# The order of the last query/key chunk and the third quarter's units in local attention

## The chip, the cores and the metric

The kernel runs on one core of a Trainium2 chip. The metric is the device time of one execution in microseconds, taken as the median over several runs. A core has TensorE (matrix products and transposes into PSUM), VectorE (DVE), ScalarE (ACT), GpSimd (POOL) and SyncE (SP). Each engine works through its own instruction list in order, and waits on semaphores for the others. Loads and stores are issued from SP's or GpSimd's queue and run on 16 shared DMA engines.

## The reference, cut to what matters

The program is a two-layer encoder trunk on 512 tokens of width 1024: a dilated sliding-window attention layer, a gated MLP, a gated linear attention layer, another MLP. The change touches the attention layer alone. It has three groups of 16 heads of width 64, with window and dilation (128, 1), (512, 4), (2048, 16):

```python
qkv = (h @ w_in).reshape(bsz, seq, A_N_GROUPS, 3, A_HEADS, A_HEAD_DIM)
for g, (window, dilation) in enumerate(A_GROUPS):
    q = rope(rms_norm(qkv[:, :, g, 0], q_gain[g]), positions)
    k = rope(rms_norm(qkv[:, :, g, 1], k_gain[g]), positions)
    o, lse = dilated_window_attention(q, k, qkv[:, :, g, 2], window, dilation)
    ...
alpha = jax.nn.softmax(jnp.stack(lses, axis=0), axis=0)
out = jnp.sum(alpha[..., None] * jnp.stack(outs, axis=0), axis=0)
return out.reshape(bsz, seq, A_WIDTH) @ w_out
```

So for each head the three groups' results are weighted by their softmax denominators, summed, and projected by `w_out`.

## The kernel before

**Quarters.** The heads are taken in four quarters of four heads. First the two dilated groups are computed for all four quarters (`attend_dilated`); their results go to DRAM. Then the local group (window 128, dilation 1) is computed for quarters 0 to 3, combined with the dilated results, and projected. The change is in this second part, in `attention` (L834 to L860).

**A query/key chunk, QK0 to QK3** (`qk_chunk`, L558). Each computes query and key of one quarter for all 512 tokens. `chunk_of` (L533) loads four weight tiles of 512 KB on SP's queue (L103), splits each in two parts on ScalarE and VectorE (L96, L97), and multiplies: 8 steps of the width, 4 token tiles, 3 products each (L547 to L549), so 96 matmuls of 512 columns into four PSUM accumulators (tag "pp", four in all). Then, token tile by token tile, ScalarE copies the accumulator to a "zs" buffer (L569) and squares it (L571), VectorE sums (L572), scales and rotates it (L585 to L590) and transposes 32x32 blocks into another "zs" buffer (L591). Sixteen transfers on SP's queue (L595) put the blocks in place in a third "zs" tile, and four ScalarE copies (L604) make the operands. There are only two "zs" buffers:

```python
"zq": 3, "qk": 8, "v": 8, "zs": 2,
```

so a tile takes its place when the tile before in that buffer has been read for the last time. QK0 to QK2 end in "zq" buffers, QK3 in four "qk" ones.

**A value chunk** (`v_chunk`, L608). For quarters 0 and 1 there is one chunk of 512 columns, and for quarters 2 and 3 a half chunk each: V2 and V3, two weight loads and 96 matmuls of 256 columns, into the same four "pp" accumulators; ScalarE copies them out (L616).

**The units, U0 to U3** (`attend_local`, L748). A quarter has four units (two pairs of heads, two pairs of token tiles). A unit is: 8 score matmuls (L767); on VectorE masking and minimum (L625); on ScalarE the exponentials (L626); 8 transposes on TensorE (L638); copies out (L656); and 16 matmuls with the values (L678). The last of these are given out one unit later (`weigh_pending`, L681). The pair's result is copied, turned back (L696), combined with the dilated one on VectorE (`combine`, L778) and turned once more (L696) to be an input of the projection, again some units later. GpSimd loads the dilated results (L751, L754) and clears borders (L628, L630).

**The output projection** (`out_attention`, L869). Its first half needs the outputs of quarters 0 and 1 (8 output tiles of 4 steps, 96 matmuls of 512 columns, L108 to L110, weights `a_w_out`), its second half also those of quarters 2 and 3. The outputs of quarters 0 and 1 are split into "xs" buffers (L852), which are those of the layer's normalized input; so the splits wait until V3, the last reader of that input, has passed.

**What sets the order.** The program is written as one sequence. A planner in the language lays it out as one list per engine before anything runs: place in the written sequence is priority, an instruction whose inputs the planner expects later is passed by later ones that it holds ready, and weight loads with their splits are given a place some hundred instructions ahead (`high_priority(offset=AHEAD)`, L103 to L105). On the chip the lists are fixed. So work that is written behind a quarter's units fills TensorE between them.

Of the kernel before, what the change touches and what calls it, by code (L numbers as in the profile page):

```python
# [39 lines left out]
class Trunk:  # L40
# [793 lines left out]
    def attention(self):  # L834
        self.masks = None
        self.pending = None
        self.later = []
        with self.phase("attn", self.ATTN):
            self.ready = self.first_tiles()
            far = [self.attend_dilated(u) for u in range(4)]  # L840
            self.load_x("xT", 64)
            qk = [self.qk_chunk("qk", 0)]
            v = [self.v_chunk(self.ins["a_w_v0"], 8)] * 2
            self.o = []
            self.inputs_read = False
            for u in range(2):
                qk.append(self.qk_chunk("qk", u + 1))
                self.attend_local(u, *qk[u], v[u], *far[u])
            for u in (2, 3):
                v.append(self.v_chunk(self.ins["a_w_v0b"][u - 2], 8, 256))  # L850
                if u == 3:
                    self.o = [self.split(e, (P, S), "xs", "xs") for e in self.o]  # L852
                    self.inputs_read = True
                self.attend_local(u, *qk[u], v[u], *far[u])
                if u == 2:
                    qk.append(self.qk_chunk("qk", 3))
            while self.pending or self.later:
                self.run_later()
                self.weigh_pending()
            self.load_h(self.ins["xT"], None)  # L860
# [363 lines left out]
```

## Time and profile before

| what | before |
|---|---|
| median of three runs | 1502.98 us (1502.92 to 1504.03) |
| the profiled execution | 1505.45 us |
| its span, first to last instruction | 1503.7 us |
| granted TensorE clock over the span | 0.994 |
| TensorE busy | 1473.7 us |
| VectorE / ScalarE / GpSimd busy | 964.3 / 785.5 / 110.2 us |

The span is the time between the first and the last instruction of the profiled execution; some 2 us lie around it. Times in rows of the profile are counted from the span's start. In rows of engines, the first number is the start, the second the length, "L" the line of the kernel, then what is written and read, shapes, and the number of instructions put together; in brackets stands how long the engine had stood idle, and what released it. "PE" is TensorE. In groups, behind the bar, stand the total busy time in us and the mean in ns, then the idle time before.

### The profile page before, as it was taken

How to read it: one execution, taken by the hardware profiler on the slowest of the kernel's cores; microseconds unless marked ns; L12 is line 12 of the kernel's file. 1: busy time of each engine (PE TensorE's matmuls, PEld its weight loads, DVE VectorE, ACT ScalarE, POOL GpSimd, SP SyncE). 2: the span in 40 equal slices, each digit the busy share in tenths (PEclk: the TensorE clock that was granted, in tenths of full speed). 3: DMA queues.
4: the chain of work that ended last, by engine and by line, in shares of the span. 5: the costliest groups of instructions: out<-in, count | busy, mean ns of one | idle time of the engine just before them, and what ended most of it. 6: DMA issues, size and time to landing. Idle time of an engine off the chain costs nothing.

```text
span 1503.7 us, 21140 instructions
## 1 busy us (share of the span) xinstructions
PE 1473.7 (98%) x7950; PEld 1209.9 (80%) x7950; DVE 964.3 (64%) x1756; ACT 785.5 (52%) x1352; POOL 110.2 (7%) x192
## 2 busy tenths in 40 slices
PE   8999999999999979999999999999999999999998
PEld 6877878777787857788888887888888888889887
DVE  6585858687775847866667334947576866668222
ACT  6334454555566355765567223556644855568121
POOL 0001010101001001111110000000010211110000
PEclk9999999999999989999999999999999999999999
DMA  8644443444333327777674333212155776675331
GB/s 275 180 126 109 123 115 95 137 145 102 110 95 106 76 68 207 224 167 154 147 157 131 99 97 99 87 56 85 50 159 184 198 168 153 156 152 148 121 107 60
DMA packets 87477, 196.53 MB, mean 131 GB/s; under 512 B 13104, under 2 KB 38256, under 8 KB 87376
## 3 DMA queue, kind: packets, MB, share of 16 engines
q1 hardware_dynamic: 72560, 145.77, 31.7%
q0 software_dynamic: 14816, 49.42, 16.2%
q8 instruction: 62, 1.02, 0.3%
q14 instruction: 39, 0.32, 0.1%
HBM read 174.11 MB, written 8.46 MB: 121 GB/s over the span
## 4 chain that ended last, share of the span: by engine, by line
PE 73%; DVE 12%; ACT 4%; DMA 4%; issue 4%; SPq 2%; POOL 0%; DVEq 0%; ACTq 0%; POOLq 0%
PE ppp L109 8%; PE ppp L108 8%; PE ppp L110 8%; PE ppp L328 6%; PE ppp L330 6%; PE ppp L329 6%; PE ppp L547 5%; PE ppp L548 5%; PE ppp L549 5%; DVE wl L97 3%; PE ps L329 2%; PE ps L330 2%; PE ps L328 2%; SPq L595 2%; PE po L678 2%
## 5 line engine op out<-in xcount | busy, mean ns | idle before, releaser
L96 ACT ACTIVATE wh<-wf 128x1024 fp32r<-128x1024 f32 (+1 forms) x184 | 191.3, 1041 | 340.8 <-PE ppp L109 187.0
L97 DVE TENSOR_TENSOR wl<-wf,wh 128x1024 fp32r<-128x1024 f32 (+1 forms) x184 | 220.4, 1199 | 206.7 <-ACT wh L96 206.1
L547 PE MATMUL ppp<-wh,xs 128*128 128x512 f32 (+1 forms) x672 | 259.1, 386 | 7.5 <-ACT wh L96 5.4
L548 PE MATMUL ppp<-wl,xs 128*128 128x512 f32 (+1 forms) x672 | 257.7, 384 | 0.1
L549 PE MATMUL ppp<-wh,xs 128*128 128x512 f32 (+1 forms) x672 | 256.3, 382 | 0.0
L547 PEld LDWEIGHTS ppp<-wh,xs 128*128 128x128 f32 x672 | 126.8, 189 | 36.4 <-ACT zs L569 5.7
L548 PEld LDWEIGHTS ppp<-wl,xs 128*128 128x128 f32 x672 | 126.9, 189 | 25.6 <-issue 2.0
L549 PEld LDWEIGHTS ppp<-wh,xs 128*128 128x128 f32 x672 | 127.0, 189 | 24.5 <-issue 0.8
L97 DVE TENSOR_TENSOR wl<-wA,wh 128x1024 fp32r<-128x1024 f32 x88 | 107.4, 1222 | 33.8 <-ACT wh L96 33.6
L96 ACT ACTIVATE wh<-wA 128x1024 fp32r<-128x1024 f32 x88 | 93.1, 1059 | 58.1 <-PE ppp L330 37.9
L328 PE MATMUL ppp<-wh,a 128*128 128x512 f32 (+1 forms) x288 | 109.1, 384 | 1.9 <-DVE h L867 1.9
L329 PE MATMUL ppp<-wl,a 128*128 128x512 f32 (+1 forms) x288 | 108.0, 375 | 0.0
L330 PE MATMUL ppp<-wh,a 128*128 128x512 f32 (+1 forms) x288 | 108.0, 376 | 0.0
L109 PE MATMUL ppp<-xs,wh 128*128 128x512 f32 x272 | 106.5, 393 | 0.0
L110 PE MATMUL ppp<-xs,wl 128*128 128x512 f32 x272 | 105.4, 390 | 1.1 <-DVE wl L97 1.1
L108 PE MATMUL ppp<-xs,wh 128*128 128x512 f32 x272 | 105.5, 392 | 0.5 <-ACT xs L96 0.5
L97 DVE TENSOR_TENSOR wl<-wB,wh 128x1024 fp32r<-128x1024 f32 x38 | 46.6, 1225 | 76.0 <-ACT wh L96 76.0
L626 ACT ACTIVATE sm<-sm,st 128x160 f32<-128x160 f32 (+2 forms) x128 | 56.9, 446 | 38.0 <-DVE st L625 37.9
L328 PE MATMUL ps<-wh,sh 128*128 128x512 f32 (+1 forms) x192 | 72.9, 381 | 0.0
L328 PE MATMUL ppp<-wh,sh 128*128 128x512 f32 (+1 forms) x192 | 72.2, 376 | 0.0
L329 PE MATMUL ps<-wl,sh 128*128 128x512 f32 (+1 forms) x192 | 71.7, 373 | 0.0
L329 PE MATMUL ppp<-wl,sh 128*128 128x512 f32 (+1 forms) x192 | 71.5, 372 | 0.1
(325 smaller groups left out, 2928.3 us busy)
## 6 DMA issues: line engine op xcount, KB each, us to landing
wA<-in_gate_up_dram POOLq DMA_DIRECT2D x52, 512.0 KB, 6.1
wf<-in_down_dram SPq DMA_DIRECT2D x32, 512.0 KB, 3.5
wf<-in_gate_up_dram SPq DMA_DIRECT2D x24, 512.0 KB, 5.2
wf<-in_a_w_v_dram SPq DMA_DIRECT2D x20, 512.0 KB, 3.9
wB<-in_gate_up_dram POOLq DMA_DIRECT2D x20, 512.0 KB, 5.6
wf<-in_a_w_q_dram SPq DMA_DIRECT2D x16, 512.0 KB, 4.0
zq<-zs SPq DMA_DIRECT2D x128, 64.0 KB, 2.1
wf<-in_a_w_qk_dram SPq DMA_DIRECT2D x16, 512.0 KB, 4.3
```

Of the source, the lines that this page charges most:

```text
L96: nc.scalar.activation(hi, src, AF.Copy)
L97: self.low = nc.vector.tensor_sub(lo, src, hi.bitcast(F32))
L108: mm(out, lhsT=wh, rhs=xh, start=start, stop=False)
L109: mm(out, lhsT=wh, rhs=xl, start=False, stop=False)
L110: self.multiplied = mm(out, lhsT=wl, rhs=xh, start=False, stop=stop)
L328: mm(a, lhsT=xh[:, tok], rhs=wh[:, f], start=start and k == 0, stop=False, skip_group_check=True)
L329: mm(a, lhsT=xh[:, tok], rhs=wl[:, f], start=False, stop=False, skip_group_check=True)
L330: self.multiplied = mm(a, lhsT=xl[:, tok], rhs=wh[:, f], start=False, stop=k == last, skip_group_check=True)
L547: mm(a, lhsT=xh, rhs=wh[:, f], start=k == 0, stop=False)
L548: mm(a, lhsT=xh, rhs=wl[:, f], start=False, stop=False)
L549: self.multiplied = mm(a, lhsT=xl, rhs=wh[:, f], start=False, stop=k == KT - 1)
L626: nc.scalar.activation(sm[:, w], sm[:, w], AF.Exp, bias=n, scale=-1.0, accum_out=l)
```

## The change

In the local part the written order of chunks and units is another. Before: QK0, V0/V1, then QK1, U0, QK2, U1, then V2, U2, QK3, V3, U3. After: QK0, V0/V1, then QK1, U0, QK2, U1, QK3, V2, U2, V3, U3. The four loop passes have one form: next query/key chunk, the half value chunk for quarters 2 and 3, the units. No instruction is added or removed.

```diff
             v = [self.v_chunk(self.ins["a_w_v0"], 8)] * 2
             self.o = []
             self.inputs_read = False
-            for u in range(2):
-                qk.append(self.qk_chunk("qk", u + 1))
-                self.attend_local(u, *qk[u], v[u], *far[u])
-            for u in (2, 3):
-                v.append(self.v_chunk(self.ins["a_w_v0b"][u - 2], 8, 256))
+            for u in range(4):
+                if u < 3:
+                    qk.append(self.qk_chunk("qk", u + 1))
+                if u > 1:
+                    v.append(self.v_chunk(self.ins["a_w_v0b"][u - 2], 8, 256))
                 if u == 3:
                     self.o = [self.split(e, (P, S), "xs", "xs") for e in self.o]
                     self.inputs_read = True
                 self.attend_local(u, *qk[u], v[u], *far[u])
-                if u == 2:
-                    qk.append(self.qk_chunk("qk", 3))
```

## The prediction

> **What bounds the kernel now.** I read the top of the profile's page first, then the waits of TensorE over the whole span.
>
> ```profile
> span 1503.7 us, 21140 instructions
> PE 1473.7 (98%) x7950; PEld 1209.9 (80%) x7950; DVE 964.3 (64%) x1756; ACT 785.5 (52%) x1352; POOL 110.2 (7%) x192
> ```
>
> ```profile
> PE ps L638 <- ACT sm L626: 7.1, 5, 4.7
> ...
> PE ps L767 <- ACT qk L604: 2.0, 1, 2.0
> ...
> PE ppp L110 <- DVE wl L97: 1.1, 1, 1.1
> ```
>
> TensorE is the bound: 1473.7 of 1503.7 us. An edit that only changes the order can win no more than its idle time and what it loses to a lowered clock. The columns of the waits are total us, times, longest. The longest single line of that list, 7.1 us, is a transpose of attention probabilities (L638) that waits for its exponentials (L626); next to it stand the first local scores (L767) that wait for a copied query and key (L604). Both lie in the part of the kernel that the change reorders. Here is that part by stretches: length, then busy us of TensorE, its weight loads, VectorE, ScalarE, GpSimd, then the granted TensorE clock.
>
> ```profile
> core 0: us, PE busy (x) PEld busy (x) DVE busy (x) ACT busy (x) POOL busy (x), PEclk, DMA share, GB/s
> 427.70:463.30 35.60, 35.13 (x279) 29.59 (x277) 30.87 (x96) 25.37 (x67) 2.34 (x8) 1.00 0.31 74
> 463.30:491.50 28.20, 27.84 (x203) 21.34 (x201) 13.24 (x53) 19.92 (x55) 2.65 (x10) 1.00 0.27 92
> 491.50:503.80 12.30, 12.30 (x101) 12.15 (x100) 12.10 (x32) 7.89 (x17) 0.99 (x3) 1.00 0.09 23
> 503.80:527.20 23.40, 22.27 (x98) 17.77 (x96) 17.23 (x29) 3.88 (x5) 0.00 (x0) 1.00 0.47 114
> 527.20:561.60 34.40, 25.80 (x187) 20.22 (x187) 16.19 (x61) 19.99 (x53) 1.44 (x6) 0.80 0.21 68
> ...
> 582.00:600.00 18.00, 17.66 (x68) 13.83 (x69) 15.46 (x25) 11.86 (x19) 1.05 (x2) 0.91 0.57 143
> 600.00:640.00 40.00, 38.48 (x173) 30.34 (x173) 35.38 (x53) 28.95 (x43) 7.82 (x12) 1.00 0.72 210
> ```
>
> With the names of the text above (QK = query/key chunk, V = value chunk, U = the four local units of a quarter): the first stretch is U1 with V2 and the start of QK3 between its units; the second is U2 with the rest of QK3; the third is V3 alone; the fourth is the first half of the output projection, all 96 of its matmuls; the fifth is U3. U1 and U2 keep TensorE at 99%, because other matmuls run while a unit's softmax is on VectorE and ScalarE. U3 does not: it loses 34.40 - 25.80 = 8.60 us, and its clock is 0.80.
>
> Why U3 has nothing to run beside it is in the time at which QK3 becomes usable. Four rows of TensorE, two of ScalarE (start, length, line), and the transfer issues of SP:
>
> ```profile
> 427.60 0.39 PE L549 MATMUL ppp<-wh,xs 128*128 128x512 f32 x1
> ...
> 492.07 0.40 PE L549 MATMUL ppp<-wh,xs 128*128 128x512 f32 x1
> ...
> 529.15 1.65 PE L767 MATMUL ps<-qk,qk 64*128 64x192 f32 x8 [1.99 <-ACT qk L604]
> 535.46 1.97 PE L638 MATMUL ps<-ident,sm 128*128 128x128 f32 x8 [4.66 <-ACT sm L626]
> ```
>
> ```profile
> 462.98 2.19 ACT L604 ACTIVATE zq<-zs 128x512 f32<-128x512 f32 x4 [0.38 <-DMA zs<-zs]
> ...
> 527.43 2.19 ACT L604 ACTIVATE qk<-zs 128x512 f32<-128x512 f32 x4 [8.21 <-DMA zs<-zs]
> ```
>
> ```profile
> 438.54 2.02 SPq L103 DMA_DIRECT2D wf<-in_a_w_qk_dram  x2
> 450.64 10.77 SPq L595 DMA_DIRECT2D zs<-zs  x16
> 461.52 1.01 SPq L103 DMA_DIRECT2D wf<-in_a_w_v0b_dram  x2
> 470.49 42.86 SPq L103 DMA_DIRECT2D wf<-in_a_w_out_dram  x5
> 514.84 10.94 SPq L595 DMA_DIRECT2D zs<-zs  x16
> ```
>
> From a chunk's last matmul to its last copy is one long chain: norm, rotation, sixteen SP transfers, four copies. For QK2 it runs from 427.99 to 465.17 (37.2 us), for QK3 from 492.47 to 529.62 (37.2 us again). Behind QK3's last matmul stand only V3 and the projection's first half, 12.3 + 23.4 = 35.7 us. They are spent as cover for the chain, and are missing when U3 comes.
>
> **The change part by part.** It removes and adds no instruction. It moves QK3 (4 weight loads, 96 matmuls, its ScalarE and VectorE chain, 16 transfers, 4 copies) from behind U2 to ahead of V2 and U2; V2 moves behind QK3, and V3 stays ahead of U3. I take its effect in the order of time.
>
> *U1.* Its filler was V2 and a part of QK3; now it is QK3.
>
> ```profile
> L547 PE MATMUL ppp<-wh,xs 128*128 128x256 f32 x32 | 9.2, 292 | 0.1
> ...
> L547 PE MATMUL ppp<-wh,xs 128*128 128x512 f32 x13 | 5.2, 399 | 0.0
> ```
>
> These are the first of three equal lines (L547, L548, L549) in 427.7 to 463.3: V2's 96 matmuls and 39 of QK3's. V3's like 96 fill the third stretch with four others, so a half value chunk is about 11.5 us. The projection's 96 of 512 columns, with two others, are the 22.27 us busy of the fourth stretch, so QK3 is about 22 us, and its 39 are 9 us. U1 took 11.5 + 9 = 20.5 us of filler; QK3 has 22. So U1 runs as before, and QK3 ends some 1.5 us behind U1, at about 464.8. Cost: nothing, with QK3 as the work that hides it; if that cover were gone, U1 would look like U3.
>
> *The hand-over from QK3 to V2.* All four accumulators of QK3 must be copied out (L569) into a "zs" buffer before V2 can start. There are two such buffers; the one QK3 needs is held until QK2's sixteen transfers have landed, at about 462.6 by the row that ends at 461.41 and the copies that start at 462.98. QK3 ends at 464.8, 2 us later. The same hand-over from QK2 to V2 before cost well under 0.5 us (the first stretch idles 0.47 us in all). I put 0.5 us on it, between 0 and 2.2 (one set of four copies, as in L604's row).
>
> *U2.* QK3's chain is now beside U2, as QK2's was beside U1: VectorE was busy 30.87 of 35.60 us there, and 13.24 of 28.20 in U2. So U2 gets U1's pace, 35.6 us in place of 28.2, and takes U1's 20.5 us of filler. There are V2 and V3, 23 us. U2 ends near 500.4; V3's last 2.5 us bring TensorE to about 503, and QK3's copies end at 464.8 + 37.2 = 502.0. The work of TensorE from 427.7 to 503.8 is the same set of instructions as before, and it stood still for only 0.83 us in it, so this point comes at 503.8 again, give or take 0.5.
>
> *U3.* Its scores are now ready when V3 ends, and the projection's first half (22 us) and 24 matmuls of its second (5 to 6 us) can go between its units and behind the last. U2 took 59 matmuls, 13.5 us, at the pace of a quarter without a chain beside it:
>
> ```profile
> L548 PE MATMUL ppp<-wl,xs 128*128 128x512 f32 x20 | 8.0, 402 | 0.0
> ...
> L108 PE MATMUL ppp<-xs,wh 128*128 128x512 f32 x8 | 3.4, 420 | 0.0
> ```
>
> (the first is one of three such lines, 20 + 20 + 19, in 463.3 to 492.3; the second one of three in 527.2 to 561.5, the 24). So 27 us are twice what U3 needs. What goes: the 8.60 us of the fifth stretch, and the lowered clock in it. For that the rows of slow groups, beside the same groups at full clock:
>
> ```profile
> 427.91 1.03 PE L767 MATMUL ps<-zq 64*128 64x192 f32 x8
> 489.03 1.06 PE L638 MATMUL ps<-ident,sm 128*128 128x128 f32 x8
> 489.93 0.60 PE L696 MATMUL pt<-ident,ob 128*128 128x128 f32 x4
> 490.46 1.09 PE L678 MATMUL po<-pt,v 128*64 128x128 f32 x16
> ...
> 537.22 1.06 PE L696 MATMUL pt<-ident,ob 128*128 128x128 f32 x4
> 538.21 1.77 PE L678 MATMUL po<-pt,v 128*64 128x128 f32 x16
> ...
> 549.49 1.63 PE L638 MATMUL ps<-ident,sm 128*128 128x128 f32 x8 [1.79 <-ACT sm L626]
> 550.92 1.06 PE L696 MATMUL pt<-ident,ob 128*128 128x128 f32 x4
> 551.91 1.76 PE L678 MATMUL po<-pt,v 128*64 128x128 f32 x16
> ```
>
> Scores 1.65 - 1.03 = 0.62; first unit's turn 1.97 - 1.06 = 0.91, 1.06 - 0.60 = 0.46, 1.77 - 1.09 = 0.68; third unit's 0.57 + 0.46 + 0.67 = 1.70. Together 4.4 us. (The mean clock of 0.80 over 25.80 busy us would allow 5.2.)
>
> [...]
>
> *The projection's first half.* Its 1.1 us wait for a weight split on VectorE (L110 on L97) I leave as it is: U3's softmax is now on that engine in place of QK3's chain, so it can be better or worse.
>
> *Behind attention.* U3's scores come some 25 us earlier (504 for 529), so what waits for its buffers starts earlier against TensorE. From 582 to 640 TensorE idles 0.34 + 1.52 us and has a clock of 0.91 for 18 us (1.6 us). I count none of it; as bounds, 3.5 us better, or the same 3.5 worse.
>
> Sum: 8.60 + 4.4 - 0.5 = 12.5 us saved. The profiled execution took 1505.45 us in all (span 1503.7); less 12.5 that is 1492.95. The median of the runs is 1502.98, 2.5 lower than that execution, so the forecast is 1502.98 - 12.5 = 1490.5.
>
> **The rivals.**
>
> *U2 runs out of filler.* V2 and V3 leave 2.5 us to spare. If the chain beside U2 makes it slower than U1, or the planner spends V3 early, TensorE idles in U2: the projection can't step in before V3 has freed the input tiles. For it: the margin. Against: U1's stretch is the same pattern, with 0.47 us idle. Price: U3's first gaps, 1.99 + 4.66 and the slow groups behind them, 2.7, come back there; 12.5 - 9.3 = 3 saved: 1500.
>
> *The transfers don't move.* The sixteen transfers stand in SP's one queue with weight loads that wait for buffers:
>
> ```profile
> SPq L103 <- DVE wl L97: 61.7, 8, 26.5
> ```
>
> The longest of those waits is 26.5 us. QK3's transfers are due 22.4 us behind its last matmul, as before (514.84 - 492.47), at 487.2. With such a load ahead of them they'd start at 487.2 + 26.5 = 513.7, about where they start now, and U3 keeps its gaps: 1503, no change. Against: before, none stood ahead of QK2's transfers in such a way; they were issued right behind VectorE's last block.
>
> *Slower: the accumulators wait for QK2's transfers.* The same wait ahead of QK2's transfers (issued from 450.64). Before, a late QK2 had all of QK3's matmuls as cover. Now QK3's accumulators can't be copied out until those transfers have landed, V2 can't start without accumulators, and U2's scores wait for the same data: TensorE has nothing. It decides from 2 us of delay (464.8 - 462.6), and costs more than the gain from 14.5. With 26.5 us: 24.5 idle, some 2 at a low clock, less 12.5, is 14 slower: 1517. For it: QK3's own loads now stand near QK2's transfers. Against: the row at 438.54 shows two of QK3's loads ahead of them already, and nothing was late.
>
> **How the numbers follow.** Forecast 0.70, with a range of its own of 1486 to 1495 (3.5 either way from what is behind attention and 1 from the hand-over); U2 without filler 0.12; transfers not moved 0.08; slower 0.10. No change is what lies within 0.2%, 3 us, about what a measurement of this kernel can tell. Faster 0.70 + 0.12 = 0.82, same 0.08, slower 0.10. The range goes from 1484.5, 1.5 below the likeliest case's own, to 1503.5, and leaves out the slower case and the tails.
>
> **What would show it.** QK3's sixteen transfers issued near 487 and not 514.8; L767 with "qk,qk" at 502 to 506; the projection's matmuls between U3's units; L638's wait below 1.5 us; a clock of 1.00 throughout 500 to 550. The forecast is wrong if TensorE idles over 3 us between 460 and 505, or if the wait moves to L767 or L547, or if 560 to 640 gives the gain back.

## The result, and the profile after

| | before | after |
|---|---|---|
| median of the runs compared | 1503.49 us (1502.92 to 1504.03) | 1487.55 us (1484.98 to 1489.99) |
| span of the profiled execution | 1503.7 us | 1483.2 us |
| TensorE busy | 1473.7 us | 1465.1 us |

The ratio of the times is 0.9894, with a 95% interval of 0.9876 to 0.9911: the change saves 15.9 us, between 13.4 and 18.6. The forecast was 12.5 saved, at 1490.5.

The top of the page after, and the waits of TensorE in it (total us, times, longest):

```profile
PE 1465.1 (99%) x7950; PEld 1206.7 (81%) x7950; DVE 965.8 (65%) x1756; ACT 786.0 (53%) x1352; POOL 110.3 (7%) x192
```

```profile
PE ps L767 <- ACT zq L604: 2.7, 1, 2.7
...
PE ps L638 <- ACT sm L626: 1.3, 2, 1.0
```

Before, L638 stood there with 7.1 us, L767 with 2.0 behind "qk", L110 with 1.1. L110 and "qk" are gone, and there is a new line: L767 waits 2.7 us for "zq". These are the stretches of the prediction in the kernel after:

```profile
427.70:463.30 35.60, 34.84 (x229) 27.34 (x227) 30.28 (x91) 21.72 (x58) 3.34 (x11) 1.00 0.37 97
463.30:491.50 28.20, 26.04 (x215) 24.36 (x216) 25.50 (x65) 19.95 (x47) 0.30 (x2) 1.00 0.25 74
491.50:503.80 12.30, 11.16 (x106) 9.50 (x105) 6.12 (x27) 8.72 (x26) 1.30 (x5) 1.00 0.56 132
503.80:527.20 23.40, 23.16 (x177) 17.83 (x176) 17.29 (x63) 18.46 (x55) 2.44 (x9) 1.00 0.24 68
527.20:561.60 34.40, 34.40 (x185) 28.36 (x186) 24.00 (x42) 13.95 (x23) 6.74 (x10) 1.00 0.80 224
561.60:582.00 20.40, 20.40 (x92) 16.89 (x91) 18.22 (x29) 13.33 (x19) 0.86 (x1) 1.00 0.27 88
582.00:600.00 18.00, 18.00 (x84) 14.89 (x82) 17.61 (x26) 14.71 (x22) 5.18 (x9) 1.00 0.98 312
600.00:640.00 40.00, 40.00 (x185) 32.47 (x185) 24.77 (x32) 25.48 (x34) 5.18 (x6) 1.00 0.66 138
```

Take the first number behind the comma from the length, and set it against the rows of before. The idle time of 8.60 us in 527.2 to 561.6 is 0, and the clock there is 1.00 for 0.80. The three stretches ahead of it got worse: from 427.7 to 503.8 TensorE idles 0.76 + 2.16 + 1.14 = 4.06 us, where it idled 0.83. The fourth went from 1.13 to 0.24. And what lies behind attention got better: from 561.6 to 640 there is no idle time left. Before, it was 2.01 in the row below, and 0.34 + 1.52 in the two rows of the prediction. (The execution after is 15 to 20 us further on in its list there, so the same times hold later work; the points behind the row compare like with like.)

```profile
561.60:582.00 20.40, 18.39 (x83) 14.45 (x82) 13.52 (x23) 8.93 (x16) 5.69 (x9) 1.00 0.85 261
```

Three points in TensorE's list place the gain between the two profiled executions. They are U0's first scores, the first gate/up product of the MLP (L328), and the MLP's first transposes (L353). First the kernel before, then the one after:

```profile
391.30 1.03 PE L767 MATMUL ps<-zq 64*128 64x192 f32 x8
...
582.06 0.47 PE L328 MATMUL ppp<-wh,a 128*128 128x512 f32 x1 [1.62 <-DVE h L867]
...
631.43 0.30 PE L353 MATMUL pt<-ident,g 128*128 128x128 f32 x1 [1.35 <-DVE g L410]
```

```profile
389.14 1.03 PE L767 MATMUL ps<-zq 64*128 64x192 f32 x8
...
567.00 0.39 PE L328 MATMUL ppp<-wh,a 128*128 128x512 f32 x1
...
611.69 0.49 PE L353 MATMUL pt<-ident,g 128*128 128x128 f32 x3
```

At U0's scores the execution after is 2.2 us ahead, though TensorE's list is the same in both kernels up to there: that is the spread of executions, not the change. (In a run below that keeps the order before, with half of QK3's transfers on another queue, these scores stand at 389.02.) From there to the first gate/up product it gains 15.1 - 2.2 = 12.9 us, from there to L353 another 19.7 - 15.1 = 4.7, and 0.8 in the 870 us that follow.

This is how the quarter's end looks now on TensorE, and on ScalarE and SP:

```profile
465.45 1.02 PE L767 MATMUL ps<-zq 64*128 64x192 f32 x6 [2.71 <-ACT zq L604]
...
482.58 1.03 PE L638 MATMUL ps<-ident,sm 128*128 128x128 f32 x8
...
502.66 1.06 PE L638 MATMUL ps<-ident,sm 128*128 128x128 f32 x8 [1.01 <-ACT sm L626]
...
505.13 1.50 PE L767 MATMUL ps<-qk,qk 64*128 64x192 f32 x8
```

```profile
462.78 1.06 ACT L96 ACTIVATE wh<-wf 128x1024 fp32r<-128x1024 f32 x1 [3.30 <-PE ppp L549]
463.75 2.17 ACT L604 ACTIVATE zq<-zs 128x512 f32<-128x512 f32 x4
...
502.42 2.17 ACT L604 ACTIVATE qk<-zs 128x512 f32<-128x512 f32 x4
```

```profile
488.08 11.02 SPq L595 DMA_DIRECT2D zs<-zs  x16
```

The signs that the prediction named are there: QK3's transfers at 488.08, U3's scores at 505.13 with no wait, no wait of L638 in U3. Two of the signs that it named for being wrong are there as well: from 460 to 505 TensorE is busy for 41.14 of 45 us, so it idles 3.86, over the 3 that were named, and a wait has moved to L767, at U2's first scores (465.45). The forecast of the time held in spite of them.

### The profile page after: what moved, and what is told of

Its sections match the earlier page's. It is cut to its first block, busy times and chain, and to the rows that moved or that the text cites. A ratio compares the mean times of both kernels' runs of the same rounds, so it can differ in the third digit from the quotient of the medians.

```text
span 1483.2 us, 21138 instructions
## 1 busy us (share of the span) xinstructions
PE 1465.1 (99%) x7950; PEld 1206.7 (81%) x7950; DVE 965.8 (65%) x1756; ACT 786.0 (53%) x1352; POOL 110.3 (7%) x192
## 4 chain that ended last, share of the span: by engine, by line
PE 78%; DVE 10%; issue 4%; ACT 4%; DMA 3%; SPq 1%; POOL 0%; ACTq 0%; DVEq 0%; POOLq 0%
PE ppp L108 9%; PE ppp L110 9%; PE ppp L109 9%; PE ppp L547 6%; PE ppp L548 6%; PE ppp L549 6%; PE ppp L328 5%; PE ppp L329 5%; PE ppp L330 5%; DVE wl L97 3%; PE ps L330 2%; PE ps L328 2%; PE ps L329 2%; PE po L678 2%; SPq L595 1%
## 5 line engine op out<-in xcount | busy, mean ns | idle before, releaser
L549 PE MATMUL ppp<-wh,xs 128*128 128x512 f32 (+1 forms) x672 | 256.2, 382 | 0.0
L549 PEld LDWEIGHTS ppp<-wh,xs 128*128 128x128 f32 x672 | 126.9, 189 | 24.6 <-issue 0.8
L328 PE MATMUL ppp<-wh,a 128*128 128x512 f32 (+1 forms) x288 | 108.2, 381 | 0.0
L110 PE MATMUL ppp<-xs,wl 128*128 128x512 f32 x272 | 106.0, 391 | 0.0
L328 PE MATMUL ps<-wh,sh 128*128 128x512 f32 (+1 forms) x192 | 73.1, 381 | 0.0
L328 PE MATMUL ppp<-wh,sh 128*128 128x512 f32 (+1 forms) x192 | 72.2, 376 | 0.0
L330 PE MATMUL ppp<-wh,sl 128*128 128x512 f32 (+1 forms) x192 | 71.6, 373 | 0.0
```

What stands on the lines that cost most here:

```text
L110: self.multiplied = mm(out, lhsT=wl, rhs=xh, start=False, stop=stop)
L328: mm(a, lhsT=xh[:, tok], rhs=wh[:, f], start=start and k == 0, stop=False, skip_group_check=True)
L330: self.multiplied = mm(a, lhsT=xl[:, tok], rhs=wh[:, f], start=False, stop=k == last, skip_group_check=True)
L549: self.multiplied = mm(a, lhsT=xl, rhs=wh[:, f], start=False, stop=k == KT - 1)
```

## The experiments

All ratios are to the kernel before, timed beside it on the same chip (its medians there were 1502.8 to 1503.8).

### Forty more products as cover for QK3's chain

If U3 loses time for want of cover, any other work ahead of it is cover too. Forty products of 512 columns, whose results nobody reads, are put between V3 and U3, into the kernel before and into the one after:

```diff
+    def idle_products(self, count):
+        ps = self.p("pp")
+        x = self.x[KT - 1][0]
+        for n in range(count):
+            self.nc.tensor.matmul(ps, lhsT=x[:, 64:192], rhs=x[:, 64:576], start=n == 0, stop=n == count - 1)
...
                 if u == 3:
+                    self.idle_products(40)
```

> The order before, with 40 products of 512 columns more, whose results nobody reads, written between V3 and U3. Cover theory (the chain of QK3 must be covered; whatever covers it is lost as filler for U3): 40 products are 9.1 us; the last 18 of the projection's first half then come between U3's units, 10 in each gap; U3's idle 8.6 us and the 4.4 us of lowered clock go, so the kernel gets FASTER by 3 to 8 us in spite of the added work (1495 to 1500). Rival theory (TensorE's work sets the time, and U3's gaps have another cause, such as transfers or ScalarE): 9 us slower, 1512.

> The changed order with the same 40 products more, in the same place. Cover theory: nothing is left to cover there, so they cost their own 9.1 us, less the 1 us that U3's first scores waited: 1495.5 to 1497. Rival theory (U3 is still held by its softmax chain, and filler is short in the changed order too): less than 4 us slower than the changed kernel, below 1492.

In the kernel before: 1498.38 us (1496.43 to 1502.22), ratio 0.9969 [0.9955, 0.9982]. TensorE has 9.1 us more to do (an estimate: 40 at the 0.227 us that each of the 98 in the 22.27 us of the projection's first half took), and the kernel is 5.1 us faster. In the kernel after: 1495.45 us (1494.32 to 1500.75), ratio 0.9953 [0.9935, 0.997], 7.9 us slower than the 1487.55 without them, and at the lower end of what was expected. The stretches and U3's first scores in the kernel before with the products:

```profile
527.20:561.60 34.40, 33.40 (x240) 25.48 (x239) 19.95 (x68) 18.31 (x51) 4.22 (x11) 1.00 0.26 89
561.60:582.00 20.40, 18.31 (x73) 14.35 (x72) 16.04 (x28) 12.79 (x21) 4.04 (x6) 0.92 0.95 247
```

```profile
529.01 1.03 PE L767 MATMUL ps<-qk,qk 64*128 64x192 f32 x8
```

The projection now fills U3's gaps, and its scores and first transposes start without a wait: cover is what U3 lacked. The second stretch shows what the products don't cure: TensorE still idles 2.1 us in 561.6 to 582, at a clock of 0.92. So there is a second loss in the kernel before, and lack of cover in U3 isn't its cause.

### Half of QK3's transfers from another queue

```diff
-                nc.sync.dma_start(turned[32 * b:32 * b + 32, :, a].rearrange("p c i j -> p c (i j)"),
+                queue = nc.scalar if kind == "qk" and u == 3 and b % 2 else nc.sync
+                queue.dma_start(turned[32 * b:32 * b + 32, :, a].rearrange("p c i j -> p c (i j)"),
```

> The order before, but half of QK3's sixteen transfers are issued from ScalarE's queue instead of SP's, nothing else. Cover theory: QK3's chain ends some 5.5 us earlier (8 issues of 0.68 us less); TensorE's wait of 1.99 us for the first scores goes, and the planner leaves 6 of the projection's matmuls (1.4 us) for U3's first gap; the clock drops less. 3 to 5 us faster, 1498.5 to 1500.5. Rival (the length of the chain doesn't matter, only the place of U3 against the projection in the written order): no change, 1503.

Measured: 1494.06 us (1492.73 to 1495.22), ratio 0.9942 [0.9921, 0.9963], 9.4 faster, twice what was expected.

```profile
512.46 6.13 SPq L596 DMA_DIRECT2D zs<-zs  x8
...
512.86 6.06 ACTq L596 DMA_DIRECT2D zs<-zs  x8
```

```profile
523.32 1.03 PE L768 MATMUL ps<-qk,qk 64*128 64x192 f32 x8
526.81 1.09 PE L639 MATMUL ps<-ident,sm 128*128 128x128 f32 x8 [0.87 <-ACT sm L627]
```

Two queues of eight issue in 6.1 us what one issued in 10.9. That took the wait of 1.99 at U3's scores, and since part of the projection was then left for the first gap, 3.8 of the 4.66 behind them, with the slow groups behind that gap. I had priced the first part alone. A chain 5 us shorter is worth nearly twice its length here, because the lowered clock goes with the idle time it removes: in 527.2 to 561.6 TensorE idles 2.45 us for 8.60, at a clock of 0.95 for 0.80.

### The order after with V2 ahead of QK3, and with the copies ahead of the split

The new wait of 2.71 us is in the ScalarE rows above. QK2's four copies (463.75) stand in ScalarE's list behind the split of V3's first weight tile (462.78). The split had to wait 3.30 us for a "wh" buffer, which QK3's last product (L549) freed. Two kernels bear on that, and the order after is run again beside them:

> The changed kernel once more, as the measure for the three beside it and for the part of the difference that lies ahead of the change. Expected: 1485 to 1490, as timed. The first 425 us have the same instruction lists in both kernels; the 2.2 us by which the profiled execution was shorter there are chance if this profile shows another number.

1487.08 us (1484.45 to 1490.92), ratio 0.9898 [0.988, 0.9916].

The first of the two writes V2 ahead of QK3 (U1, V2, QK3, U2, V3, U3):

```diff
             for u in range(4):
+                if u == 2:
+                    v.append(self.v_chunk(self.ins["a_w_v0b"][0], 8, 256))
                 if u < 3:
                     qk.append(self.qk_chunk("qk", u + 1))
-                if u > 1:
-                    v.append(self.v_chunk(self.ins["a_w_v0b"][u - 2], 8, 256))
+                if u == 3:
+                    v.append(self.v_chunk(self.ins["a_w_v0b"][1], 8, 256))
```

> The changed order, but V2 written ahead of QK3 (U1, V2, QK3, U2, V3, U3). Theory (the place of QK3 ahead of U2 is what matters; the 2.7 us that TensorE waited at 462.75 come from QK3's accumulators and U2's scores both waiting for QK2's transfers): QK3 ends some 11 us later, QK2's chain is long done, the wait goes; the projection gives 46 matmuls as cover for QK3's chain and still has 10 for each gap of U3. 1 to 3 us faster than the changed kernel, or 2 slower at worst if U3's first scores come late. Rival (QK3 must be ahead of V2 too): 5 us or more slower than the changed kernel.

Measured: 1481.77 us (1481.55 to 1481.89), ratio 0.9863 [0.9847, 0.9878]. That is 5.3 us better than the order after, where 1 to 3 were expected, and the fastest kernel of this study.

```profile
463.30:503.80 40.50, 40.06 (x285) 33.68 (x283) 32.69 (x92) 27.68 (x69) 1.59 (x7) 1.00 0.25 67
```

```profile
473.50 1.03 PE L767 MATMUL ps<-zq 64*128 64x192 f32 x8
```

U2's scores follow QK3's last product (473.58) at once: QK2's chain now has V2 and QK3 as cover. The idle time of 463.3 to 503.8 falls from 2.16 + 1.14 to 0.44, by 2.9 us. The rest of the 5.3 goes along with the clock, as far as its means of three digits tell. The order after took 1484.45 and 1485.31 us in its executions at a mean granted clock of 1.000, and 1490.92 in one at 0.997; with V2 first all four ran at 0.999 or 1.000, within 0.4 us of each other.

The second keeps the order after, but V3's loads and splits may not pass QK2's copies:

```diff
+                if u == 1:
+                    copied = self.last_copy
...
+                if u == 3:
+                    with self.tc.issue_after(copied.ins):
+                        v.append(self.v_chunk(self.ins["a_w_v0b"][1], 8, 256))
```

> The changed order, but the split of V3's weights is kept behind QK2's four copies on ScalarE, where it had stood ahead of them and waited for a weight buffer until QK3's last matmul. Theory: U2's scores come 1.6 us earlier, the wait of 2.7 us shrinks to about 1; 1 to 2 us faster than the changed kernel. Rival (the wait is the length of QK2's chain of transfers, the split stands in it by accident): no difference.

Measured: 1485.46 us (1484.36 to 1488.26), ratio 0.989 [0.9872, 0.9908].

```profile
463.36 2.19 ACT L604 ACTIVATE zq<-zs 128x512 f32<-128x512 f32 x4 [3.52 <-DMA zs<-zs]
```

```profile
462.72 0.39 PE L549 MATMUL ppp<-wh,xs 128*128 128x512 f32 x1
465.08 1.02 PE L767 MATMUL ps<-zq 64*128 64x192 f32 x6 [1.97 <-ACT zq L604]
```

The copies now start as QK2's transfers land, and the wait at L767 is 2.0 us in place of 2.7, where about 1 was expected. So the split was the smaller part of it. The rest is the copies' own time, 2.19 us, behind transfers that land when QK3's products are over (463.36, against 462.72 + 0.39 = 463.11). The 1.6 us against the order after lie within the spread of the two.

### Behind attention: early loads, or where a tile lies

The kernel after gains 4.7 us between the first gate/up product and L353. My first idea was that GpSimd's loads for the MLP start 30 us earlier (532.04 for 562.20), and are out of the way. So they were held in the order after, behind a copy of one column into a new small tile:

```diff
-    FFN = {"Rc": 4, "wB": 2, "a": NH - KT}
+    FFN = {"hold": 1, "Rc": 4, "wB": 2, "a": NH - KT}
...
-                    sums(nc.gpsimd)
+                    with self.tc.issue_after(self.held.ins):
+                        sums(nc.gpsimd)
...
+                    if part and t == 0 and i == 0:
+                        self.held = self.nc.gpsimd.tensor_copy(self.t("hold", (P, 1)), self.h[m][:, 0:1])
```

> The changed order, but GpSimd's first loads for the gate/up stage are put behind one small GpSimd copy that reads the output of the first product of the projection's second half, so that they start some 18 us ahead of the gate/up products, as before (20 us), in place of 35. If the gain behind attention (about 4.6 us between 582 and 631 us of the span before) came from loads that start earlier: 4 us or more slower than the changed kernel. If it came from VectorE, which got the second half's sums one by one and not in a burst: within 1 us of the changed kernel.

Measured: 1492.38 us (1491.48 to 1496.87), ratio 0.9933 [0.9917, 0.9949], 5.3 slower. That fitted the idea, but the profile didn't: TensorE had no new wait behind attention, at a clock of 1.00. Instead its products of the first MLP came further apart. Three more kernels part the load from the tile. The first holds the loads as above, with a tile of 512 bytes for each partition in place of 4, `self.t("hold", (P, 128))[:, 0:1]`:

> The order after, with the first gate/up loads of the MLP held until the projection's second half has its first product (near 555 us of the span, where they started near 532), as in the run with held loads before it; only the small extra tile is now 512 bytes wide for each partition in place of a few. Theory A (the loads' early start is worth nothing behind attention, and the 5.3 us of that run came from where the extra tile put the MLP's buffers): the 512-wide matmuls of the first MLP, 580 to 930 us, come again every 0.227 us in place of 0.233; 1486 to 1489 us, within 2 us of the order after. Theory B (the held loads themselves slow the MLP): 1491 to 1493 us, and the spacing of 0.233 stays.

The second has the tile of 4 bytes and the copy, and holds no load; the third is the second with a tile of 64 bytes, `(P, 16)`:

> The order after, with the same small extra tile and the one small GpSimd copy into it as in the run with held loads, but with no load held. Theory A (the place of the MLP's buffers sets the pace): 512-wide matmuls every 0.233 us from 580 to 930 us, and 1490 to 1493 us. Theory B (the held loads set it): 0.227 us, and 1486 to 1489 us.

> The run with the small extra tile again (no load held), with a tile of 64 bytes for each partition in place of 4. Theory A (what costs is that the MLP's buffers begin at a place that is no multiple of 64 bytes): weight loads 0.227 us apart from 820 to 930 us, and 1486 to 1489 us. Theory B (a coarser measure counts: only the tile of 512 bytes keeps the pace): 0.233 us apart, and 1490 to 1494 us.

| order after, and | us | ratio |
|---|---|---|
| loads held, tile of 4 bytes | 1492.38 | 0.9933 [0.9917, 0.9949] |
| loads held, tile of 512 bytes | 1486.80 | 0.9889 [0.9874, 0.9904] |
| loads not held, tile of 4 bytes | 1492.47 | 0.9929 [0.9916, 0.9941] |
| loads not held, tile of 64 bytes | 1490.71 | 0.9920 [0.9897, 0.9944] |

The held loads cost nothing: 1486.80 against 1487.08 without them. The tile costs 5 us, by its size alone. TensorE's weight loads in the MLP's down projection, first with the tile of 512 bytes, then with that of 4:

```profile
869.85 0.19 PEld L108 LDWEIGHTS ppp<-wA,wh 128*128 128x128 f32 x1
...
872.12 0.19 PEld L109 LDWEIGHTS ppp<-wB,wh 128*128 128x128 f32 x1
```

```profile
870.00 0.19 PEld L109 LDWEIGHTS ppp<-g,wh 128*128 128x128 f32 x1
...
872.10 0.19 PEld L109 LDWEIGHTS ppp<-g,wh 128*128 128x128 f32 x1
```

Between the first two rows lie ten steps, 2.27 / 10 = 0.227 us each; between the next two nine, 2.10 / 9 = 0.233. With 64 bytes the step is 0.229 here; that kernel's interval meets both that of the tile of 4 bytes and that of the order after, so the times alone don't place it. The first kernel of this set, then, says nothing of loads, and the idea of their early start falls. That the tile acts by where the buffers behind it begin is argued, since its size alone differs and no trace shows addresses; which of these buffers counts wasn't tried.

### Behind attention: VectorE's sums in a bunch

```diff
+        for pair in ((0, 1), (2, 3)):
+            open_sums = []
+            for t in pair:
+                w = self.weight(self.ins["a_w_out"][1, t], 1024)
                 for i, m in enumerate((half + t, t)):
+                    open_sums.append((t, i, m, w, self.p("pp")))
+            for ks in ((0, 1), (2, 3)):
+                for t, i, m, w, ps in open_sums:
...
```

> The order after, but the projection's second half opens four accumulators at once: steps 0 and 1 for all four, then 2 and 3, so that VectorE gets its sums four close together, as in the kernel before, where this half's last steps waited for the fourth quarter. Theory A (behind attention the kernel before lost its time because VectorE got these sums in a bunch, and the first gate/up products waited for them): a wait of 1 to 2 us of TensorE for the normalized input (L328 of the order after) or at the first down products comes back, with a lowered clock behind it; 1489 to 1492 us. Theory B (what was won there is the loads' earlier start, or nothing of the order within the projection): 1486.5 to 1488.5 us, no such wait.

Measured: 1488.15 us (1486.32 to 1490.41), ratio 0.9898 [0.9885, 0.9912], and no wait at L328. A bunch of this kind isn't the cause. But it is a loose one: VectorE's first two sums start 1.36 us apart here (553.48 and 554.84), as their accumulators end, while in the kernel before four accumulators end 0.45 us apart (last products at 567.81, 568.26, 568.72 and 569.17). The run of the next part keeps that tight bunch.

### Behind attention: a weight split ahead of the sums

Then I followed the wait of 1.62 us at L328 back in the kernel before. ScalarE, VectorE, and GpSimd's and SP's transfers from 562 to 582 us (KB each, median us from issue to landing):

```profile
578.20 1.06 ACT L96 ACTIVATE wh<-wf 128x1024 fp32r<-128x1024 f32 x1 [3.12 <-DMA wf<-in_gate_up_dram]
```

```profile
579.29 1.23 DVE L97 TENSOR_TENSOR wl<-wf,wh 128x1024 fp32r<-128x1024 f32 x1 [3.06 <-ACT wh L96]
...
581.23 0.69 DVE L867 TENSOR_TENSOR h<-ppp,h 128x512 f32<-128x512 f32 x1
```

```profile
wA<-in_gate_up_dram POOLq DMA_DIRECT2D x7, 512.0 KB, 6.8
wf<-in_gate_up_dram SPq DMA_DIRECT2D x3, 512.0 KB, 7.3
wB<-in_gate_up_dram POOLq DMA_DIRECT2D x2, 512.0 KB, 8.2
```

```profile
575.00:580.00 5.00, 5.00 (x23) 4.14 (x23) 1.94 (x4) 1.89 (x4) 0.00 (x0) 1.00 1.03 418
```

Twelve transfers of 512 KB share these 20 us, and at 575 to 580 they move 418 GB/s at a DMA share of 1.03. The split of the second gate/up tile waits for one of them, 3.12 us, in ScalarE's list ahead of the projection's last block sums. VectorE's half of the split waits behind it, and behind that stands the add that empties an accumulator (L867, 581.23), which L328 needs. The next kernel moves this split alone, in the kernel before, behind the second pair's block sums:

```diff
             load(0, "wf")
-            return ready("wf")
+            w = [self.split(raw["wf"][0], (P, 1024), "wh", "wl")]
+            with self.tc.issue_after(self.anchor.ins):
+                w.append(self.split(raw["wf"][1], (P, 1024), "wh", "wl"))
+            return w
...
                     self.pair_sums(t)
+                    if t == 1:
+                        self.anchor = self.on_act
```

> The kernel before, with one split moved: that of the second weight tile of the first gate/up product stands on ScalarE and VectorE behind the block sums of the projection's second pair of outputs (it stood ahead of them, and waited 3.12 us there for its load). Its load keeps its time. Theory A (behind attention the kernel before lost its time because this split waits for a load that shares the DMA engines with nine others of 512 KB, and the sums that free the accumulators are queued behind it): VectorE's idle time of 3.06 us near 576 to 579 is gone, TensorE's first gate/up product no longer waits 1.84 us for them, the lowered clock from 582 to 600 goes with it; 1498.5 to 1501 us, 2.5 to 5 us faster than before. Theory B (the load itself is what TensorE is short of, or the sums are late for another reason): the wait goes to the split weight or stays at the sums, and the time is within 1 us of before, 1502.5 to 1504.5.

(The 1.84 us in that text is the wait at L328 in the run with the forty products; in the kernel before it is 1.62.)

Measured: 1497.73 us (1496.18 to 1501.28), ratio 0.9959 [0.9945, 0.9972], 6.1 us faster (4.2 to 8.3), where theory A had 2.5 to 5.

```profile
580.17 1.06 ACT L96 ACTIVATE wh<-wf 128x1024 fp32r<-128x1024 f32 x1 [0.58 <-DMA wf<-in_gate_up_dram]
```

```profile
582.05 0.39 PE L334 MATMUL ppp<-wh,a 128*128 128x512 f32 x1
...
627.75 0.38 PE L359 MATMUL pt<-ident,g 128*128 128x128 f32 x2
```

```profile
582.00:600.00 18.00, 17.79 (x77) 13.81 (x77) 17.36 (x28) 12.10 (x19) 3.04 (x4) 1.00 0.64 155
```

The first gate/up product (here L334) follows the projection without a wait (this execution's last transposes of U3 came 1.8 us later than in that of before, which is why its start is the same). The clock behind it is 1.00, and from it to the first transposes it is 45.7 us, where it was 49.4 before and 44.7 after. Theory A stands in its mechanism, at more than its price: the loss is the split's place in two lists, ahead of the sums, while its load is late. The tight bunch of sums is still there, so it isn't the cause. That the load is late because it shares the DMA engines is the author's reading of the row at 418 GB/s and a DMA share of 1.03; no run changed that alone. In the kernel after both are otherwise. The projection runs on without U3's gaps, so SP's loads are issued one by one as its weights free their buffers, and GpSimd's have gone before. These are its transfers from 547 to 567 us, the 20 us ahead of its first gate/up product:

```profile
wf<-in_gate_up_dram SPq DMA_DIRECT2D x4, 512.0 KB, 5.2
wA<-in_gate_up_dram POOLq DMA_DIRECT2D x2, 512.0 KB, 7.2
```

Six where there were twelve, and the weights land 5.2 us after their issue, for 7.3.

## Why the prediction was right, and where it was not

**U3: right.** The 8.60 us and the lowered clock (4.4) are gone: U3 now starts at 505.13, in a stretch with 0.24 us idle and a clock of 1.00. The forty products show that lack of cover was the cause, and with cover its scores don't wait and the clock is 1.00. (The view that the prediction quotes for the projection's second half counts 8 + 7 + 7 = 22 products up to 561.5, where it says 24; nothing hangs on it.)

**U1 and the transfers: right.** QK3 filled U1, and its transfers went out at 488.08 (487 was forecast). No weight load held them, so the rival "the transfers don't move" did not come.

**The hand-over from QK3 to V2: mis-sized.** It was priced at 0.5 us, at most 2.2, as a wait for QK2's transfers. TensorE stood still for 2.71. The forecast had the transfers land 2 us ahead of QK3's end. In the run with the copies first they landed 0.25 us behind it: counted from U1's first scores (425.97 there), they were issued 1.3 us later than in the kernel before and released ScalarE 2.3 us later. (In the kernel before, too, they released it at 462.98; the forecast's 462.6 is where ScalarE fell idle.) And behind the transfers stand QK2's copies: U2's scores read them, and in ScalarE's list they are ahead of the copies of QK3's accumulators (L569, at 465.82 in the kernel after). So the 2.2 us that I took as an upper end were due nearly in full, 1.97 in that run, and the split ahead of them in ScalarE's list added the rest. This is the slower rival in small, the same wait without a load that holds the transfers. With V2 ahead of QK3 the wait goes.

**U2: nearly right.** U2 took more filler than U1 had: its first transposes came at 482.58, 17 us behind its scores, since VectorE, busy for 25.50 of 28.20 us there, had QK3's chain first. V3 lasted until the last gap, where 1.01 us were missing. The rival "U2 runs out of filler" came true to that size, and not to its 9.3. Hand-over and filler together made 4.06 us idle in place of 0.83, so 3.2 where the sum had 0.5.

**The wait at L110**, left as it was, is gone: 0.9 in that stretch.

**Behind attention: the term that failed.** It was counted as nothing, with 3.5 either way. By the stretches it gave 2.01 + 0.34 + 1.52 us of idle time and 1.6 of lowered clock, 5.5 in all. I took a shift in time to do no more than move the waits about. But the place of a load against others is part of the order too, and a split late by 3.12 us held the sums.

The sum by what was measured, between the profiles: 8.60 + 4.4 - 3.2 + 0.9 + 5.5 = 16.2, against 12.5 forecast and 15.9 between the medians. The errors of 2.7 (hand-over and U2) and 6.4 (L110 and behind attention) have opposite signs, so the forecast was nearer than its terms, and that is luck. That 16.2 comes so near 15.9 is chance too: the profiled execution of before lies 2.0 us above its median, that of after 2.6 below. What remains of the 20.5 us between the two profiled executions is the 2.2 ahead of U0, some 1.2 between the first gate/up product and L353 that no idle time shows, and 0.8 later.

**The clock.** In the profiled execution of the kernel before it was 0.50 in three stretches between 500 and 600 us, one of 10.2 us and two of about 3.4, a third of that (the 3.4 us on either side of each show 0.99 or 1.00):

```profile
529.40:539.60 10.20, 5.54 (x34) 4.49 (x34) 4.25 (x11) 6.20 (x14) 0.30 (x2) 0.50 0.44 139
...
549.90:553.30 3.40, 3.40 (x25) 3.07 (x25) 0.66 (x1) 1.79 (x3) 0.15 (x1) 0.50 0.00 0
...
584.10:587.40 3.30, 3.30 (x9) 2.58 (x8) 3.27 (x7) 2.63 (x5) 0.00 (x0) 0.50 1.01 199
```

If work at a clock of 0.50 takes twice as long, as the transposes at 535.46 nearly did (1.97 us for 1.06), a stretch costs half its busy time: 5.54 / 2 + 3.40 / 2 = 4.5 in U3, an estimate that agrees with the prediction's 4.4, and 3.30 / 2 = 1.7 behind attention. The stretches begin 20.5 and 34.2 us apart, about six and ten times 3.4, so in this execution the three starts fit one grid. The gap of 1.79 us lies ahead of the second. The longer gap of 2.71 us in the kernel after left the clock at 1.00, while behind the same wait of 2.7 us in the run with the tile of 64 bytes (466.14) it was 0.50 for 3.3 us:

```profile
467.80:471.10 3.30, 3.30 (x17) 3.30 (x17) 3.06 (x11) 3.30 (x9) 0.00 (x0) 0.50 0.21 84
```

So the length of a gap alone does not say whether the clock falls, and what does is open here. The prediction's use of the rows for this term was borne out, since all 4.4 us went with the gaps.

## What to carry to other kernels

In this kernel a long chain (norm, transfers, copies: 37.2 us) cost its consumer what its cover lacked, 8.60 us of idle time, and a lowered clock on top, some 4.4. So count the matmul work between a chunk's end and its first reader in the written order, for every chunk, and put a piece of work between any two that hand over directly. When a shift of 20 us is planned, look at the loads that will then run at the same time, and at each engine's list for a weight split that waits for a load ahead of work that TensorE needs (here it waited 3.12 us). And when an experiment adds a tile, run the tile alone as well: here one of 4 bytes cost 5 us by itself, and one of 512 bytes nothing.

## What the runs showed of the hardware that was not expected

A tile of 4 bytes for each partition, used once, made the products of the first MLP come every 0.233 us in place of 0.227, at a granted clock of 1.00 and without a wait (from 820 to 930 us TensorE is busy for 110.00 of 110 us, with 473 matmuls in place of the 486 with the tile of 512 bytes): 1492.47 us for the kernel in place of 1487.08. With 64 bytes it was 1490.71, between the two and not clear of either, and with 512 bytes 1486.80, no loss. So here a tile that TensorE never reads had a price of 5 us, and none of TensorE's waits shows it; that the price lies in where the other buffers begin is the author's guess, not shown.
